# Hybrid attention block: logits of both heads of a pair from 64-row products, and another order of query ranges

## The chip, the core and the metric

The kernel runs on one core of one Trainium2 chip. The metric is the device time of one execution in microseconds (us). Five kinds of work appear in the profile: PE (TensorE matmuls), PEld (TensorE weight loads, which overlap PE), DVE (VectorE), ACT (ScalarE), POOL (GpSimd); SP is the queue that issues most DMAs. Lines such as L103 are lines of the kernel before; L103 is the helper through which most ordered instructions are recorded, so groups there are told apart by their tiles (`p`, `z`, `wt`, `av`).

## The reference

One layer on a (1, 1024, 1024) residual stream, 16 heads of 64 dimensions. What matters here is the attention branch, for each head and with the strictly causal mask `s < t`:

```
proj = h @ w_in            # q, k, v, z_a, u, z_b, m_a, m_b, each 1024 wide
z    = q @ k.T * 64**-0.5                                  # logits
A[t,s] = sigmoid(z_ts) * prod_{s<j<t} (1 - sigmoid(z_tj))  # stick breaking
p_a  = ((A @ v) * silu(z_a)) @ w_branch_a
```

Beside it runs a pooling branch (`u`, `z_b`, `w_branch_b`). Both are gated by `sigmoid(m_a)` and `sigmoid(m_b)`, summed, projected by `w_out`, added to `x`, and normed.

## The kernel before, in words

All inputs are float32. A product keeps the accuracy by splitting each operand in a high and a low part (type fp32r, "hi" and "lo"), and adding hi·hi, hi·lo and lo·hi in the same PSUM bank; that is three TensorE products of 128 rows and up to 512 columns for each 128 rows of depth.

The sequence is kept in reversed order, so that query block `qb` (128 queries) meets the keys from `qb*128` to the end, a width W of 1024, 896, 768, 640, 512, 384, 256 or 128 columns. A unit of attention is (p, h, t): one of 8 head pairs p, head h of the pair, query range t of two blocks (256 queries). W is cut in chunks of up to 512 columns, so a head has 4, 4, 2 and 2 chunks in t = 0, 1, 2, 3: four of 512 columns, five of 384, two of 256 and one of 128.

For each chunk `z_items` (it begins near L800) makes:

- the logits in a PSUM bank with the tag `z` (two banks);
- on ACT two sigmoids out of the bank, `om` = sigmoid(-z) (L819) and `be` = sigmoid(z) (L820);
- on POOL the causal mask of the first 128 columns of both (L824);
- after the last chunk of a block, on DVE, the running product of `om` (the scan, L826), and, put off until the next `flush`, `be` times the shifted running product (an ordered multiplication, recorded under L103). `be` then holds the attention weights of 128 queries.

`turn` transposes these weights 128x128 at a time on TensorE (`wt`, two PSUM banks with the tag `tr`), copies them to hi and lo (L845 on ACT, L846 on DVE) and flushes what was put off. `product` multiplies them with v (`av`), and `finish` (L870 to L876) adds up the parts, multiplies with silu(z_a) and stores to DRAM (`ga_d`).

A logit product of one head has only 64 rows of depth. The kernel before fills all 128 rows: for head 0 the tile `q0` holds q-hi in rows 0 to 63 and q-lo in rows 64 to 127; `kh` holds k-hi twice, above and below; `kl` holds k-lo in one half and zeros in the other. Then q0·kh is hi·hi + lo·hi in one product, and q0·kl is hi·lo. So a chunk of a head takes two products. Making these tiles takes moves from one half of the partitions to the other: 3 DMAs for each half-sequence of q (`use_q`), 5 for each of k (`use_k`), all issued on SP by `move` (L697), and 4 memsets on POOL (L678).

Between these pieces stand the projections. `fill(n)` emits n steps of the generator `projections`, each three products of 512 columns (`p`). Each pair has the k, the q, 0 to 2 gate and the z_a column tiles. `step` interleaves the logits of the units that come due, the transposes and av products of the current unit, and a share of the 70 steps of each pair (`QUANTA`, `SHARE`). The logits of a unit are made three units ahead (`LEAD`), and units are taken in the order `HT_ORDER`: (0,0), (0,2), (1,0), (1,2), (0,1), (0,3), (1,1), (1,3). Everything that is emitted through `order` in this stage keeps its program order on its engine; the rest (sigmoids, scans, copies) is placed by a scheduler at build time.

Of the kernel before, what the change touches and what calls it, by code (L numbers as in the profile page):

```python
# [30 lines left out]
Z_TAGS = ("z",)  # L31
# [26 lines left out]
def block_kernel(ctx, tc, a, out):  # L58
# [613 lines left out]
    with pool("at") as at:  # L672
        pair = {}

        klz = [atz.tile([P, 2, S], F32R, name=f"kl{i}") for i in range(2)]
        for t_ in klz:
            for h in range(2):
                gp.memset(t_[64 * (1 - h):64 * (1 - h) + 64, h].bitcast(F32), 0.0)  # L678

        def pair_tiles(p, use):  # L680

            def tile_(tag, shape, dt=F32R, pl=atz):
                return pl.tile([P] + shape, dt, tag=tag, bufs=2, name=f"{tag}_{p}")

            if use is use_k:
                pair[p] = dict(kh=tile_("kh", [2, S]), kl=klz[p % 2])
            elif use is use_q:
                pair[p]["q"] = [tile_(f"q{h}", [S]) for h in range(2)]
            elif use is use_za:
                pair[p].update(vv=tile_("vv", [8, 2, 2, HD], pl=at), za=tile_("za", [S], F32, at))  # L690
# [5 lines left out]
        def move(dst, src):  # L696
            nc.sync.dma_start(dst.bitcast(F32), src.bitcast(F32))  # L697

        def low(name, ps, hi):
            lo = atz.tile([P, 512], F32R, tag="lo", bufs=1, name=name)  # L700
            order(v.tensor_sub)(lo, ps, hi.bitcast(F32))
            return lo

        def use_q(p, sh, ps):
            (q0, q1), sl = pair[p]["q"], slice(sh * 512, sh * 512 + 512)
            act.copy(q0[:, sl], ps)
            lo = low(f"qlo{p}_{sh}", ps, q0[:, sl])
            move(q1[half(1), sl], q0[half(1), sl])
            move(q1[half(0), sl], lo[half(1)])
            move(q0[half(1), sl], lo[half(0)])  # L710

        def use_k(p, sh, ps):
            kh, kl, sl = pair[p]["kh"], pair[p]["kl"], slice(sh * 512, sh * 512 + 512)
            act.copy(kh[:, 0, sl], ps)

            def rest():
                lo = low(f"klo{p}_{sh}", ps, kh[:, 0, sl])
                for h in range(2):
                    move(kl[half(h), h, sl], lo[half(h)])
                move(kh[half(1), 1, sl], kh[half(1), 0, sl])  # L720
                move(kh[half(0), 1, sl], kh[half(1), 0, sl])
                move(kh[half(1), 0, sl], kh[half(0), 0, sl])

            behind.append(rest)
            if p == 0:
                flush()
# [71 lines left out]
        z_tags = cycle(Z_TAGS)  # L798

        def z_items(u):  # L800

            p, h, t = u
            st = pair[p]
            rows = unit_rows[u] = []
            for qb in (2 * t, 2 * t + 1):
                n0 = qb * P
                W = S - n0
                om = atz.tile([P, S], F32, tag="om", bufs=2, name=f"om{p}_{h}_{qb}")
                g = t // 2
                be = at.tile([P, S - 512 * g], F32, tag=f"be{g}", bufs=NBE[g], name=f"be{p}_{h}_{qb}")  # L810
                nch = (W + 511) // 512
                b0 = 0
                for i in range(nch):
                    n = -(-((W - b0) // P) // (nch - i)) * P
                    zp = bank(next(z_tags), f"z{p}_{h}_{qb}_{i}")
                    ks, qsl = slice(n0 + b0, n0 + b0 + n), slice(n0, n0 + P)
                    mm(zp[:, :n], st["q"][h][:, qsl], st["kh"][:, h, ks], start=True, stop=False)
                    mm(zp[:, :n], st["q"][h][:, qsl], st["kl"][:, h, ks], start=False, stop=True)
                    act.activation(om[:, b0:b0 + n], zp[:, :n], AF.Sigmoid, scale=-0.125)  # L819
                    act.activation(be[:, b0:b0 + n], zp[:, :n], AF.Sigmoid, scale=0.125)  # L820
                    b0 += n
                    if i == 0:
                        for tl, fill in ((om, 1.0), (be, 0.0)):
                            gp.affine_select(out=tl[:, :P], in_=tl[:, :P], pattern=[[1, P]], compare_op=ALU.is_gt, fill=fill, base=0, channel_multiplier=-1)  # L824
                    if i == nch - 1:
                        v.tensor_tensor_scan(om[:, :W], om[:, :W], om[:, :W], 1.0, ALU.mult, ALU.min)  # L826
                        behind.append(lambda be=be, om=om, W=W: order(v.tensor_mul)(be[:, 1:W], be[:, 1:W], om[:, :W - 1]))
                        rows.append(be)
# [54 lines left out]
        ahead = {}  # L883
        for i, u in enumerate(units):
            ahead.setdefault(i - LEAD[u[2]], []).append(u)
# [7 lines left out]
        def n_z(u):  # L893
            return 4 if u[2] < 2 else 2
# [9 lines left out]
        def av_items(u):  # L904
            c = chunks.index((u, u[2]))
            for kp in range(u[2], 4):
                turn_next()
                product(u, kp, *turned_[c])
                turned_[c] = None
                c += 1  # L910
                if kp == 3:
                    finish(u)
                yield

        def first_items():
            for _ in range(DEPTH):
                turn_next()
                yield

        def step(zus, i, quanta):  # L920

            zs = [(g, n) for g, n in ((z_items(zu), n_z(zu)) for zu in zus)]
            items = [g for _, g in sorted(((k + 0.5) / n, j) for j, (g, n) in enumerate(zs) for k in range(n))]
            items = [zs[j][0] for j in items]
            main, n_main = (first_items(), DEPTH) if i == -1 else (av_items(units[i]), 4 - units[i][2]) if i >= 0 else (None, 0)
            n = max(n_main, len(items))
            groups = [[] for _ in range(n)]
            for k, g in enumerate(items):
                groups[(2 * k + 1) * n // (2 * len(items))].append(g)
            for k in range(n_main):  # L930
                groups[(2 * k + 1) * n // (2 * n_main)].append(main)
            done = 0
            for k, group in enumerate(groups):
                for g in group:
                    next(g)
                upto = quanta * (k + 1) // n
                fill(upto - done)
                done = upto
            for g in [main] + [g for g, _ in zs]:
                assert g is None or next(g, None) is None  # L940
            if i < 0:
                flush()
# [3 lines left out]
        early_ = sorted(s_ for s_ in ahead if s_ < 0)  # L946
        for n, s_ in enumerate(early_):
            step(ahead[s_], s_, FIRST[1] * (n + 1) // len(early_) - FIRST[1] * n // len(early_))
        for p in range(NP):
            used = 0  # L950
            for k in range(8):
                upto = QUANTA[p] * sum(SHARE[:k + 1]) // sum(SHARE)
                step(ahead.get(p * 8 + k, []), p * 8 + k, upto - used)
                used = upto
                if p * 8 + k == max(ahead):
# [3 lines left out]
                    ga = load_ga(0, range(NP - 1))  # L959
        pinned[0] = False  # L960
# [143 lines left out]
```

## Time and profile before

| what | value |
|---|---|
| three runs | 1209.69, 1210.95, 1212.34 us; median 1210.95 us |
| profiled execution, first to last instruction | span 1210.3 us (its own time; 0.7 us under the median) |
| PE busy | 1199.2 us, 99% of the span |
| PEld busy | 1002.5 us, 83% |
| DVE, ACT, POOL busy | 756.5, 531.6, 187.2 us |
| mean granted TensorE clock | 0.999 |
| attention stage | first logit product at 415.8 us, last at 991.4 us |

The page says how long each engine was busy. A matmul row's mean time is longer than the distance from one matmul to the next, since matmuls are pipelined; the timeline's start times give the distance. Rows of the weight-load track show when the weights of a product were loaded; in a steady stream that is while the product ahead of it runs.

### The profile page before, as it was taken

Reading aid. Unit: us, or ns where it says so; the run is one execution under the profiler, and the core shown is the slowest. Engines: PE = TensorE matmul, PEld = TensorE weight load, DVE = VectorE, ACT = ScalarE, POOL = GpSimd, SP = SyncE. Lnnn points to the kernel's source line nnn. Section 1 sums busy time; section 2 is a strip of 40 time slices with the busy share of each in tenths; the row PEclk is TensorE's granted clock in tenths of the full one; section 3 lists DMA queues with packets and bytes.
Section 4 is the critical chain, followed back from the end, with each engine's and each line's share of the span. In section 5 each row is a group of like instructions: output and inputs, shape, how many; then the busy total and the mean of one; then the engine's idle time right before and its main releaser. Section 6 shows DMA issues by size and latency. Waiting matters only on the chain.

```text
span 1210.3 us, 16177 instructions
## 1 busy us (share of the span) xinstructions
PE 1199.2 (99%) x5746; PEld 1002.5 (83%) x5746; DVE 756.5 (63%) x1050; ACT 531.6 (44%) x1008; POOL 187.2 (15%) x360
## 2 busy tenths in 40 slices
PE   8999999999999999999999999999999999999997
PEld 7888878888888888888888888888888888888886
DVE  5764483677510286767868677686777853785643
ACT  5564331334301255655555555655555643232211
POOL 1000000001221333212222222222221210000001
PEclk9999999999999999999999999999999999999999
DMA  9649995626847632442635325353343344975622
GB/s 358 255 171 325 328 356 207 209 87 225 309 148 120 191 91 76 124 122 86 170 109 156 113 80 153 110 157 118 102 134 101 99 131 167 353 272 170 216 67 83
DMA packets 81955, 207.14 MB, mean 171 GB/s; under 512 B 10449, under 2 KB 23889, under 8 KB 79698
## 3 DMA queue, kind: packets, MB, share of 16 engines
q1 hardware_dynamic: 73666, 191.23, 49.2%
q10 hardware_dynamic: 8208, 14.88, 3.3%
q8 instruction: 45, 0.74, 0.2%
q14 instruction: 36, 0.29, 0.1%
HBM read 138.96 MB, written 50.34 MB: 156 GB/s over the span
## 4 chain that ended last, share of the span: by engine, by line
PE 88%; DMA 5%; issue 3%; DVE 2%; ACT 1%; POOL 0%; POOLq 0%; ACTq 0%; DVEq 0%; SPq 0%
PE p L103 34%; PE pb L103 7%; PE wzb L103 7%; PE pa L103 7%; PE o L103 6%; PE z L103 6%; PE av L103 5%; PE wt L103 5%; PE v L103 4%; PE ua L103 3%; DMA wl_d<-l_raw 2%; DMA l_raw<-in_w_in 2%; PE u L103 2%; PE wm L103 1%; DVE l_raw L156 1%
## 5 line engine op out<-in xcount | busy, mean ns | idle before, releaser
L103 PE MATMUL p<-hT,w 128*128 128x512 f32 x1920 | 480.0, 391 | 0.5 <-ACT m_sg L201 0.5
L103 PEld LDWEIGHTS p<-hT,w 128*128 128x128 f32 x1920 | 355.2, 188 | 74.7 <-ACT m_sg L201 1.0
L826 DVE TENSOR_TENSOR_SCAN om<-om 128x512 f32<-128x512 f32 (+7 forms) x128 | 175.8, 1373 | 124.9 <-ACT om L819 69.4
L819 ACT ACTIVATE om<-z 128x512 f32<-128x512 f32 (+2 forms) x192 | 94.5, 492 | 155.9 <-PE z L103 133.5
L824 POOL TENSOR_SCALAR_AFFINE_SELECT om<-om 128x128 f32<-128x128 f32 x128 | 56.3, 440 | 346.5 <-ACT om L819 287.0
L846 DVE TENSOR_TENSOR wt<-wt,wt 128x512 fp32r<-128x512 f32 (+1 forms) x160 | 99.3, 621 | 16.1 <-ACT wt L845 15.5
L845 ACT CAST wt<-wt 128x512 fp32r<-128x512 f32 (+1 forms) x160 | 88.2, 551 | 48.1 <-PE wt L103 47.9
L103 PE MATMUL av<-wt,vv 128*128 128x512 f32 x320 | 106.4, 414 | 0.0
L103 DVE TENSOR_TENSOR be<-be,om 128x511 f32<-128x511 f32 (+7 forms) x128 | 95.1, 749 | 1.1 <-POOL be L824 0.7
L820 ACT ACTIVATE be<-z 128x512 f32<-128x512 f32 (+2 forms) x192 | 94.1, 490 | 0.0
L103 PE MATMUL pa<-ga,wa 128*128 128x512 f32 x384 | 89.6, 389 | 0.1
L103 PE MATMUL o<-wo,mhl 128*128 128x512 f32 (+1 forms) x408 | 89.6, 377 | 0.0
L103 PE MATMUL wt<-ident,be 128*128 128x128 f32 x576 | 89.4, 273 | 0.0
L103 PE MATMUL v<-wv,hT 128*128 128x512 f32 x384 | 87.8, 390 | 0.5 <-DVE vo L611 0.5
L103 PE MATMUL wzb<-hT,wzb 128*128 128x512 f32 x384 | 87.2, 389 | 0.0
L103 PE MATMUL pb<-gb,wb 128*128 128x512 f32 x384 | 87.2, 389 | 0.0
L103 PEld LDWEIGHTS v<-wv,hT 128*128 128x128 f32 x384 | 71.9, 188 | 16.2 <-DVE vo L611 1.4
L103 PEld LDWEIGHTS o<-wo,mhl 128*128 128x128 f32 x408 | 73.5, 188 | 14.1
L103 PEld LDWEIGHTS pa<-ga,wa 128*128 128x128 f32 x384 | 72.0, 188 | 15.4 <-DVE wa L118 0.5
L103 PEld LDWEIGHTS wzb<-hT,wzb 128*128 128x128 f32 x384 | 72.1, 188 | 14.9
L103 PEld LDWEIGHTS pb<-gb,wb 128*128 128x128 f32 x384 | 72.1, 188 | 14.9
L103 PEld LDWEIGHTS wt<-ident,be 128*128 128x128 f32 x576 | 70.2, 141 | 11.6
(130 smaller groups left out, 1364.5 us busy)
## 6 DMA issues: line engine op xcount, KB each, us to landing
w_raw<-in_w_in SPq DMA_DIRECT2D x40, 512.0 KB, 4.7
l_raw<-in_w_in SPq DMA_DIRECT2D x32, 512.0 KB, 5.2
wl_d<-l_raw SPq DMA_DIRECT2D x32, 512.0 KB, 5.7
w<-wl_d SPq DMA_DIRECT2D x32, 512.0 KB, 3.8
v_d<-vo SPq DMA_DIRECT2D x16, 512.0 KB, 5.2
vv<-v_d SPq DMA_DIRECT2D x8, 1024.0 KB, 5.3
wa_raw<-in_w_branch_a SPq DMA_DIRECT2D x16, 512.0 KB, 4.7
wa<-in_w_mod SPq DMA_DIRECT2D x7, 1024.0 KB, 6.4
```

The source lines that it names most:

```text
L103: ins = op(*args, **kw)
L156: v.tensor_sub(raw.bitcast(F32R), raw, hi.bitcast(F32))
L819: act.activation(om[:, b0:b0 + n], zp[:, :n], AF.Sigmoid, scale=-0.125)
L820: act.activation(be[:, b0:b0 + n], zp[:, :n], AF.Sigmoid, scale=0.125)
L824: gp.affine_select(out=tl[:, :P], in_=tl[:, :P], pattern=[[1, P]], compare_op=ALU.is_gt, fill=fill, base=0, channel_multiplier=-1)
L826: v.tensor_tensor_scan(om[:, :W], om[:, :W], om[:, :W], 1.0, ALU.mult, ALU.min)
L845: act.copy(wt[:, 0, :off], pt[:, :off])
L846: v.tensor_sub(wt[:, 1, :off], pt[:, :off], wt[:, 0, :off].bitcast(F32))
```

## The change

The logits of both heads of a pair are made together. `use_q` and `use_k` keep q-hi, q-lo, k-hi, k-lo as they come out of the projection, head 0 in partitions 0 to 63 and head 1 in 64 to 127. A chunk of both heads is six products of 64 rows, hi·hi, lo·hi, hi·lo, each for head 0 in the upper half of the array's rows and for head 1 in the lower half, in two PSUM banks. The moves, the zeroed tiles and the POOL memsets go. Query ranges are taken in the order 0, 3, 1, 2, in each both heads one after the other; the logits of the next range of both heads are made during the current one, instead of three units ahead. Transposes run two chunks ahead of the av products over the whole stage (`main_items`), and the share of projection steps of each range is 15, 18, 17, 24 instead of equal eighths.

```diff
-HT_ORDER = ((0, 0), (0, 2), (1, 0), (1, 2), (0, 1), (0, 3), (1, 1), (1, 3))
-LEAD = {0: 3, 1: 3, 2: 3, 3: 3}
+T_ORDER = (0, 3, 1, 2)
+HT_ORDER = tuple((h, t) for t in T_ORDER for h in range(2))
 NBE = (4, 4)
-SHARE = (7,) * 8
+SHARE = (15, 18, 17, 24)
...
-        klz = [atz.tile([P, 2, S], F32R, name=f"kl{i}") for i in range(2)]
-        for t_ in klz:
-            for h in range(2):
-                gp.memset(t_[64 * (1 - h):64 * (1 - h) + 64, h].bitcast(F32), 0.0)
...
         def use_q(p, sh, ps):
-            (q0, q1), sl = pair[p]["q"], slice(sh * 512, sh * 512 + 512)
-            act.copy(q0[:, sl], ps)
-            lo = low(f"qlo{p}_{sh}", ps, q0[:, sl])
-            move(q1[half(1), sl], q0[half(1), sl])
-            move(q1[half(0), sl], lo[half(1)])
-            move(q0[half(1), sl], lo[half(0)])
+            (hi, lo), sl = pair[p]["q"], slice(sh * 512, sh * 512 + 512)
+            act.copy(hi[:, sl], ps)
+            order(v.tensor_sub)(lo[:, sl], ps, hi[:, sl].bitcast(F32))
...
-        def z_items(u):
+        def z_items(p, t):
+
+            (kh, kl), (qh, ql) = pair[p]["k"], pair[p]["q"]
...
-                    zp = bank(next(z_tags), f"z{p}_{h}_{qb}_{i}")
+                    zp = [bank("z", f"z{p}_{h}_{qb}_{i}") for h in range(2)]
                     ks, qsl = slice(n0 + b0, n0 + b0 + n), slice(n0, n0 + P)
-                    mm(zp[:, :n], st["q"][h][:, qsl], st["kh"][:, h, ks], start=True, stop=False)
-                    mm(zp[:, :n], st["q"][h][:, qsl], st["kl"][:, h, ks], start=False, stop=True)
-                    act.activation(om[:, b0:b0 + n], zp[:, :n], AF.Sigmoid, scale=-0.125)
-                    act.activation(be[:, b0:b0 + n], zp[:, :n], AF.Sigmoid, scale=0.125)
+                    for j, (q_, k_) in enumerate(((qh, kh), (ql, kh), (qh, kl))):
+                        for h in range(2):
+                            mm(zp[h][:, :n], q_[half(h), qsl], k_[half(h), ks], start=j == 0, stop=j == 2)
+                    for h in range(2):
+                        act.activation(om[h][:, b0:b0 + n], zp[h][:, :n], AF.Sigmoid, scale=-0.125)
+                        act.activation(be[h][:, b0:b0 + n], zp[h][:, :n], AF.Sigmoid, scale=0.125)
...
+        def main_items():
+            for c in range(len(chunks)):
                 turn_next()
+                if c >= DEPTH:
+                    use_chunk(c - DEPTH)
                 yield
...
+        def step(nxt, cur, quanta):
+
+            events = []
+            if nxt:
+                z, n = z_items(*nxt), n_z(nxt[1])
+                events += [((k + 0.2) / (n + 0.8), 0, z) for k in range(n)]
+            if cur:
+                n = 2 * (4 - cur[1])
+                events += [((k + 0.5) / n, 1, main) for k in range(n)]
```

Three places show what this does to the engines' orders. The first is TensorE, at the logits of query blocks 2 and 3 (range t = 1) of a pair. The names are `z_<head>_<block>_<chunk>`, `p_<half>`, `wt` (transposes) and `av`. Before:

```order
L103 MATMUL p_0_4965<-hT,w_13_4766 128x512 x6
L103 MATMUL z_0_2_0_4974<-kh_3899,q_2_4070 128x384
L103 MATMUL z_0_2_0_4974<-kl_2932,q_2_4070 128x384
L103 MATMUL p_0_4965<-hT,w_13_4766 128x512 x6
L103 MATMUL z_0_2_1_4989<-kh_3899,q_2_4070 128x384
L103 MATMUL z_0_2_1_4989<-kl_2932,q_2_4070 128x384
L103 MATMUL wt_1_0_0_4995<-ident,be_1_0_4775 128x128 x2
```

And in the change:

```order
L101 MATMUL z_0_2_0_5003<-kh_3854,qh_3993 128x384
L101 MATMUL z_1_2_0_5004<-kh_3854,qh_3993 128x384
L101 MATMUL z_0_2_0_5003<-kh_3854,ql_3994 128x384
L101 MATMUL z_1_2_0_5004<-kh_3854,ql_3994 128x384
L101 MATMUL z_0_2_0_5003<-kl_3855,qh_3993 128x384
L101 MATMUL z_1_2_0_5004<-kl_3855,qh_3993 128x384
L101 MATMUL p_1_5023<-hT,w_13_4720 128x512 x12
L101 MATMUL z_0_2_1_5036<-kh_3854,qh_3993 128x384
L101 MATMUL z_1_2_1_5037<-kh_3854,qh_3993 128x384
```

Two products for one head have become six for two heads, the heads taking turns. There are 96 such groups in place of 192 pairs of products, and each stands between products of 128 rows (or 128-row transposes).

The second place is DVE, at the logits of range t = 0 of the following pair, from the last scan of block 0 to the weights of block 1 (`om` is the scan, `be` the multiplication that makes the weights, `tp` an addition in `finish`, `wt` the low part of transposed weights). Before, for head 0:

```order
L826 SCALAR_TENSOR_TENSOR om_0_1_4626<-om_0_1_4626 128x896
L872 TENSOR_TENSOR tp_3_4649<-av_0_3_4646,tp_3_4649 64x256
L734 TENSOR_TENSOR za_4608<-p_0_4610,za_4608 128x512
L826 SCALAR_TENSOR_TENSOR om_0_4_4676<-om_0_4_4676 128x512
L846 TENSOR_TENSOR wt_1_1_3_4693<-wt_1_1_3_4688,wt_1_1_3_4693 128x512
L103 TENSOR_TENSOR be_0_1_4627<-be_0_1_4627,om_0_1_4626 128x895
```

And in the change, for both heads:

```order
L801 SCALAR_TENSOR_TENSOR om_0_1_5464<-om_0_1_5464 128x896
L801 SCALAR_TENSOR_TENSOR om_1_1_5465<-om_1_1_5465 128x896
L822 TENSOR_TENSOR wt_1_2_3_5549<-wt_1_2_3_5544,wt_1_2_3_5549 128x512
L101 TENSOR_TENSOR kl_5436<-p_0_5437,kh_5435 128x512
L101 TENSOR_TENSOR be_0_1_5466<-be_0_1_5466,om_0_1_5464 128x895
L101 TENSOR_TENSOR be_1_1_5467<-be_1_1_5467,om_1_1_5465 128x895
```

The scans of both heads now stand next to each other, and the weights of head 0 come after the scan of head 1. The transposes that need them, `wt_0_0_0` of the next pair, stand after 15 `p` products, four transposes, two av products and 9 more `p` products on TensorE, counted from the last logits of block 1.

The third place is ACT at the logits of block 2. Before, two sigmoids of one head follow each other (`om`, `be`), and the second of the two banks takes the next chunk. In the change:

```order
L691 CAST qh_4926<-p_0_4928 128x512
L793 ACTIVATE om_0_2_4999<-z_0_2_0_5003 128x384
L794 ACTIVATE be_0_2_5001<-z_0_2_0_5003 128x384
L793 ACTIVATE om_1_2_5000<-z_1_2_0_5004 128x384
L794 ACTIVATE be_1_2_5002<-z_1_2_0_5004 128x384
L793 ACTIVATE om_0_2_4999<-z_0_2_1_5036 128x384
```

Both banks are now filled at once, and four sigmoids empty them before the next group can begin.

More of the change, by code (lines that the diff above doesn't have):

```diff
@@ L685, in pair_tiles @@
             if use is use_k:
-                pair[p] = dict(kh=tile_("kh", [2, S]), kl=klz[p % 2])
+                pair[p] = dict(k=[tile_(n, [S]) for n in ("kh", "kl")])
             elif use is use_q:
-                pair[p]["q"] = [tile_(f"q{h}", [S]) for h in range(2)]
+                pair[p]["q"] = [tile_(n, [S]) for n in ("qh", "ql")]
             elif use is use_za:
@@ L693, in half @@
             return slice(64 * h, 64 * h + 64)
[L696 to L702, printed above, removed]
-        def use_q(p, sh, ps):
-            (q0, q1), sl = pair[p]["q"], slice(sh * 512, sh * 512 + 512)
-            act.copy(q0[:, sl], ps)
-            lo = low(f"qlo{p}_{sh}", ps, q0[:, sl])
-            move(q1[half(1), sl], q0[half(1), sl])
-            move(q1[half(0), sl], lo[half(1)])
-            move(q0[half(1), sl], lo[half(0)])
-        def use_k(p, sh, ps):
[L713 to L724, printed above, removed]
+        def use_q(p, sh, ps):
+            (hi, lo), sl = pair[p]["q"], slice(sh * 512, sh * 512 + 512)
+            act.copy(hi[:, sl], ps)
+            order(v.tensor_sub)(lo[:, sl], ps, hi[:, sl].bitcast(F32))
+        def use_k(p, sh, ps):
+            (hi, lo), sl = pair[p]["k"], slice(sh * 512, sh * 512 + 512)
+            act.copy(hi[:, sl], ps)
+            behind.append(lambda: order(v.tensor_sub)(lo[:, sl], ps, hi[:, sl].bitcast(F32)))
             if p == 0:
@@ L882, in block_kernel @@
         units = [(p, h, t) for p in range(NP) for h, t in HT_ORDER]
-        ahead = {}
-        for i, u in enumerate(units):
-            ahead.setdefault(i - LEAD[u[2]], []).append(u)
+        pairs = [(p, t) for p in range(NP) for t in T_ORDER]
         proj = projections()
@@ new lines, in main_items, with use_chunk @@
+                yield
+            for c in range(len(chunks) - DEPTH, len(chunks)):
+                use_chunk(c)
+            yield
+        def use_chunk(c):
+            u, kp = chunks[c]
+            product(u, kp, *turned_[c])
+            turned_[c] = None
+            if kp == 3:
+                finish(u)
+        main = main_items()
+        def step(nxt, cur, quanta):
[6 more added lines that the diff above has]
+                events += [((k + 0.5) / n, 1, main) for k in range(n)]
@@ L932, in step @@
             done = 0
[L933 to L936, printed above, removed]
+            for at_, _, g in sorted(events, key=lambda e: e[:2]):
+                upto = int(quanta * at_)
                 fill(upto - done)
                 done = upto
[L939 to L942, printed above, removed]
+                next(g)
@@ L944, in block_kernel @@
+            fill(quanta - done)
+            if nxt:
+                assert next(z, None) is None
         fill(FIRST[0])
         pinned[0] = True
-        early_ = sorted(s_ for s_ in ahead if s_ < 0)
-        for n, s_ in enumerate(early_):
-            step(ahead[s_], s_, FIRST[1] * (n + 1) // len(early_) - FIRST[1] * n // len(early_))
+        step(pairs[0], None, FIRST[1])
+        flush()
         for p in range(NP):
             used = 0
-            for k in range(8):
+            for k in range(4):
```

61 lines of the change are left out of this document (19 added, 42 removed).

## The prediction, made before the result was known

> **What bounds the kernel now.** I read the page's busy shares first, then the windows of single pairs, then the waits of the attention stage.
>
> ```profile
> span 1210.3 us, 16177 instructions
> PE 1199.2 (99%) x5746; PEld 1002.5 (83%) x5746; DVE 756.5 (63%) x1050; ACT 531.6 (44%) x1008; POOL 187.2 (15%) x360
> ```
>
> ```profile
> 438.00:511.00 73.00, 73.00 (x374) 61.64 (x372) 54.35 (x76) 42.62 (x90) 22.06 (x38) 1.00 0.35 97
> 876.00:949.00 73.00, 73.00 (x373) 61.60 (x372) 53.24 (x74) 41.58 (x90) 15.56 (x36) 1.00 0.40 119
> ```
>
> ```profile
> PE p L103 <- ACT m_sg L201: 0.5, 1, 0.5
> ```
>
> The window rows give PE, PEld, DVE, ACT, POOL busy in one pair's 73 us: PE all of it, DVE 54, ACT 42. Between 391 and 1030 us PE waited once, for 0.5 us. So the stage lasts as long as its TensorE stream: what is added to the stream is added to the time, and what is taken from DVE, ACT, SP or the DMAs gains nothing. A busy row doesn't say how dense the stream is, so the costs below are distances between starts.
>
> **What a logit product costs now.** The tile view of `z` counts the products (the other operand's row has the same counts), the chain has a long plain run, and three pieces of the timeline show starts.
>
> ```profile
> L103 PE MATMUL z<-kh,q x192: 220/333/389, 415.8 to 991.3; 128*128 128x384 f32 x80, 128*128 128x512 f32 x64, 128*128 128x256 f32 x32, 128*128 128x128 f32 x16
> ```
>
> ```profile
> 216.69 87.04 PE wzb L103 x384
> ```
>
> ```profile
> 512.88 0.39 PE L103 MATMUL z<-kh,q 128*128 128x512 f32 x1
> 513.11 0.39 PE L103 MATMUL z<-kl,q 128*128 128x512 f32 x1
> 513.34 0.60 PE L103 MATMUL wt<-ident,be 128*128 128x128 f32 x4
> 513.69 0.71 PE L103 MATMUL av<-wt,vv 128*128 128x512 f32 x2
> 514.24 1.55 PE L103 MATMUL p<-hT,w 128*128 128x512 f32 x6
> ...
> 517.81 0.33 PE L103 MATMUL z<-kh,q 128*128 128x384 f32 x1
> 517.98 0.34 PE L103 MATMUL z<-kl,q 128*128 128x384 f32 x1
> 518.15 0.60 PE L103 MATMUL wt<-ident,be 128*128 128x128 f32 x4
> ```
>
> ```profile
> 991.34 0.22 PE L103 MATMUL z<-kh,q 128*128 128x128 f32 x1
> 991.40 0.28 PE L103 MATMUL z<-kl,q 128*128 128x128 f32 x1
> ```
>
> 87.04/384 is 0.227 us for 512 columns. The logits keep that pace: 0.23 at 512, 0.17 at 384, 0.06 at 128, in proportion to the columns, and going into and out of them costs nothing. One pass over the logits of all heads has 64x512 + 80x384 + 32x256 + 16x128 = 73,728 columns, that is 144 x 0.227 = 32.7 us. Before there are two passes: 65.3 us.
>
> **Term 1, the products.** After the change there are three passes, with both heads at once if the two halves of the array run side by side. Then they last 3 x 32.7/2 = 49.0 us, which is **-16.3 us**. One by one they last 98.0 us, +32.7. No row shows two products side by side, since all products here but two are of 128 rows; these are the bounds. I take the first: the heads use different rows, different weights and different banks, and alternate in the order. In groups of 128 columns (8 of 96) the pace may be set by weight loads: the last two rows above show a load and its product every 0.06, so two loads make 0.11 against 0.06, and 8 x 3 x 0.06 = **+1.4 us**.
>
> **Term 2, going in and out.** The logits now stand in 96 groups, each between products of 128 rows: 192 changes. The only products of fewer rows in the trace are the spreads of `c`, `crow`, of one row, near the start.
>
> ```profile
> 8.71 1.24 PE L103 MATMUL wm<-praw,wt_raw 128*128 128x256 f32 x5
> 9.88 1.98 PE L103 MATMUL crow<-crow,ones 1*128 1x512 f32 x4
> 11.79 3.72 PE L103 MATMUL wm<-praw,wt_raw 128*128 128x256 f32 x16
> 15.35 7.07 PE L103 MATMUL wm<-praw,wt 128*128 128x256 f32 x32
> 22.25 0.93 PE L103 MATMUL xt<-ident,x 128*128 128x128 f32 x7
> ```
>
> ```profile
> 9.14 0.41 PEld L103 LDWEIGHTS wm<-praw,wt_raw 128*128 128x128 f32 x2
> 9.88 0.29 PEld L103 LDWEIGHTS crow<-crow,ones 1*128 1x128 f32 x2 [0.33 <-issue]
> 10.41 0.18 PEld L103 LDWEIGHTS crow<-crow,ones 1*128 1x128 f32 x1 [0.24 <-issue]
> 10.85 0.18 PEld L103 LDWEIGHTS crow<-crow,ones 1*128 1x128 f32 x1 [0.24 <-issue]
> 11.79 0.51 PEld L103 LDWEIGHTS wm<-praw,wt_raw 128*128 128x128 f32 x3 [0.76 <-issue]
> ```
>
> The run of 32 `wm` products gives their pace, (22.25 - 15.35)/32 = 0.216. Five from 8.71 end at 9.79, but `crow` begins at 9.88: 0.09 late. The second `crow` load starts at 9.88 + 0.29 - 0.18 = 9.99 and the fourth at 10.85, so a product takes 0.43, and four from 9.88 end at 11.60; `wm` begins at 11.79: 0.19 late. Sixteen from there would end at 15.24; the next begin at 15.35: 0.11 late. Together 0.39 us are lost on one trip in and out, and the rows say "issue": nothing the profile shows was awaited. I read it as two parts, each twice. The stream empties (0.09), and then the first weights load with nothing running (0.11, the distance of the first two `crow` loads), where otherwise the load stands beside the product ahead.
>
> [...]
>
> Carried over to 64 rows: emptying 2 x 0.09. The loads exposed are fp32r loads, which cannot take longer than the 0.06 of the rows at 991 us, against 0.11 for the fp32 loads of `crow`; 2 x 0.06. And the second head's weights load after the first head's, so its stream ends up to 0.06 later. That is 0.35 per group; its bounds are 0.18 (emptying alone) and 0.39 (as `crow`), below both 0 if 64 rows need no change of state. 96 x 0.35 = **+33.6 us** (17.3 to 37.4; rival B is 0).
>
> [...]
>
> **Term 3, the shorter lead.** Logits used to be three units ahead; now the last logits of range 0 stand just ahead of their first transposes. TensorE has 15 + 9 `p` products (5.4 us) and four transposes with two av products (0.9, as from 513.34 to 514.24) between them, 6.3 us, and 0.15 for leaving the group. Against it stands this chain on DVE, by the stage's groups by shape:
>
> ```profile
> L819 ACT ACTIVATE om<-z 128x384 f32<-128x384 f32 x80 | 39.4, 492 | 57.3 <-PE z L103 54.7 <-issue 1.6 <-ACT wt L845 0.7
> ```
>
> ```profile
> L846 DVE TENSOR_TENSOR wt<-wt,wt 128x512 fp32r<-128x512 f32 x94 | 63.3, 673 | 9.3 <-ACT wt L845 9.0
> L826 DVE TENSOR_TENSOR_SCAN om<-om 128x896 f32<-128x896 f32 x16 | 32.3, 2017 | 1.1 <-ACT om L819 0.8
> L103 DVE TENSOR_TENSOR be<-be,om 128x895 f32<-128x895 f32 x16 | 17.5, 1094 | 0.0
> L103 DVE TENSOR_TENSOR klo<-p,kh 128x512 fp32r<-128x512 f32 x14 | 9.5, 680 | 0.0
> ```
>
> Sigmoid 0.49, two scans 4.03, a `wt` low part 0.67, `be` 1.09: 6.3 us, and 0.68 more where a k low part stands between, as in the order shown. So TensorE arrives about when the weights do, and waits up to 0.5 us in the pairs with the k part: **+2 us** over the seven pairs that follow another. Bounds 0 and 5 (0.7 in each). The other ranges have some microseconds of room.
>
> **What is worth nothing.** 128 moves and four memsets go:
>
> ```profile
> kh<-kh SPq DMA_DIRECT2D x48, 128.0 KB, 3.7
> kl<-klo SPq DMA_DIRECT2D x32, 128.0 KB, 3.7
> q<-qlo SPq DMA_DIRECT2D x32, 128.0 KB, 2.4
> q<-q SPq DMA_DIRECT2D x16, 128.0 KB, 3.4
> ```
>
> They delayed other loads on SP, but PE waited for no load in the stage, so this is hidden under the TensorE stream (0; if that cover went, a load of weights would come earlier, not later). DVE and ACT do the same operations as before. The two banks of `z` are now filled together, and the next group waits for four sigmoids, 4 x 0.49 = 2.0 us, where 12 `p` products (2.7 us) stand between at the tightest: 0.
>
> **Sum.** -16.3 + 1.4 + 33.6 + 2 = +20.7. On the profiled 1210.3 (0.7 below the median, which I add back) this gives 1231.0, and 1231.7 against the median: **1232 us**, slower by 1.7%. The case's own range is 1213 (0.18 per group, no wait) to 1238.5 (0.39, 5 us of waits).
>
> **Rivals.**
>
> A is this forecast, chance 0.60.
>
> B: changing to 64 rows costs nothing. The place is the same 192 borders, and the change is faster as soon as a group's way in and out costs less than (16.3 - 1.4 - 2)/96 = 0.13 us. With 0.06 at most, for the second head's late start, the sum is -16.3 + 1.4 + 2 + 3 (half of 5.8) = -10, **1201 us**. For it: half of the rows is not one row, and the transposes between products of other kinds show no loss. Against it: `crow` waited for nothing and still lost 0.39, three times that limit. Chance 0.22, of which 0.04 near the limit, where the time is within 0.2% (2.4 us, about what a measurement of this kernel tells from no change).
>
> C: the change doesn't do what it says, and the halves run one after the other. The groups lose 0.30 (no late second head) and the products gain nothing: 32.7 + 28.8 + 2 = +63, **1274 us**; with free borders 1246. For it: no row shows two products at once. Against it: the heads share neither rows nor banks. Chance 0.13.
>
> D: the shorter lead decides. If ACT takes up a group's sigmoids 2 us later than I count, since it now has four in a row, TensorE waits 2 us at the first transposes of each of the eight pairs, 16 in place of term 3: 20.7 - 2 + 16 = +35, **1246 us**. It decides once the chain of term 3 is more than 0.2 us longer than the 6.5 us of cover. For it: DVE is at 54 of 73 us, in bursts. Against it: ACT is idle 30 of 73 us. Chance 0.05.
>
> **Numbers.** The likeliest is 1232. The range 1199 to 1252 holds A, nearly all of B, D, and C with free borders; outside stay C with its borders (about 0.1) and B's best (0.05). Faster by over 0.2%: B without its margin, 0.18. Within: 0.05. Slower: 0.77.
>
> **What would show it.** In the changed profile, the first `z` of a group should start about 0.1 us later than the `p` ahead of it allows, with its weight load at the same time, and the `p` behind likewise (term 2; none of it is B). The `z` of head 1 should start within 0.06 of head 0's, and the next product of head 0 one product time later (term 1; two product times is C). PE waits for `be` should be a few, under 1 us, at the first transposes of a pair (term 3; long or many is D). PE should stay busy with a pair's period about 2.6 us over 73. The forecast is wrong if the borders lose less than 0.13 us or the pairs of products take over 1.5 times one.

## The result, and the profile after

| | before | after |
|---|---|---|
| median | 1211.45 us (1209.69 to 1212.34) | 1262.43 us (1259.51 to 1264.86) |
| profiled execution, span | 1210.3 us | 1263.1 us |
| last `p` before the first logits to the first `pa` behind the stage | 613.5 us | 665.6 us |
| mean granted TensorE clock | 0.999 | 0.991 |

The change makes the kernel slower: ratio 1.0423, 95% interval 1.0403 to 1.0444. The forecast was slower by 20.7 us; it is 51 us. The spans of the profiled executions differ by 52.8 us, and 52.0 of that lie in the attention stage. The page of the changed kernel, its span and busy shares:

```profile
span 1263.1 us, 16295 instructions
PE 1231.6 (98%) x5938; PEld 980.3 (78%) x5938; DVE 769.9 (61%) x1050; ACT 531.8 (42%) x1008; POOL 183.2 (15%) x356
```

PE is busy 32 us longer and idle 20 us more. One pair, as the window view shows it (columns as in the prediction):

```profile
518.00:596.00 78.00, 76.47 (x399) 58.70 (x399) 54.55 (x75) 42.29 (x90) 16.52 (x36) 1.00 0.27 92
```

A pair's period went from 73 to 78 us, and in it PE is no longer busy throughout. What PE waited for is in the view of waits (us in total, times, longest):

```profile
PE av L101 <- DVE tp L848: 15.2, 8, 3.3
PE p L101 <- ACT m_sg L199: 2.5, 1, 2.5
PE wt L101 <- DVE be L101: 1.9, 3, 1.4
```

Before, the stage had one wait, 0.5 us, for `m_sg`. The third row is what the prediction had looked for; the first, eight times larger, is something that it did not look at.

**The borders.** The timeline of TensorE and of its weight loads around one group of 512 columns:

```profile
548.72 4.26 PE L101 MATMUL p<-hT,w 128*128 128x512 f32 x18
552.91 0.50 PE L101 MATMUL z<-kh,qh 64*128 64x512 f32 x2
553.25 0.40 PE L101 MATMUL z<-kh,ql 64*128 64x512 f32 x2
553.48 0.40 PE L101 MATMUL z<-kl,qh 64*128 64x512 f32 x2
553.81 0.55 PE L101 MATMUL wt<-ident,be 128*128 128x128 f32 x3
```

```profile
552.91 0.19 PEld L101 LDWEIGHTS z<-kh,qh 64*128 64x128 f32 x2 [0.35 <-issue]
553.02 0.19 PEld L101 LDWEIGHTS z<-kh,ql 64*128 64x128 f32 x2
553.25 0.19 PEld L101 LDWEIGHTS z<-kl,qh 64*128 64x128 f32 x2
553.81 0.31 PEld L101 LDWEIGHTS wt<-ident,be 128*128 128x128 f32 x3 [0.37 <-issue]
```

The view joins the two heads' products in one row ("x2"): in the trace they start 3 ns apart, so the halves do run side by side. But the first loads stand at the same time as the first products (552.91 and 552.91, again at 553.81): nothing was loaded ahead. From 552.91 the next product comes after 0.34 (0.11 over a product of 0.23), then after 0.23, then the border out after 0.33 (0.10 over). The medians over all groups of 512 columns, by starts: 0.318 from the last `p` to the first `z` (0.091 over 0.227), 0.332 to the second, 0.230 to the third, 0.323 to a following `p` (0.096 over), and 0.337 to the `p` after that (0.110 over). Together that is 0.40 us per group.

**The wait for a bank.** Two units later, TensorE and DVE:

```profile
558.76 0.60 PE L101 MATMUL wt<-ident,be 128*128 128x128 f32 x4
560.89 0.58 PE L101 MATMUL av<-wt,vv 128*128 128x512 f32 x2 [1.53 <-DVE tp L848]
```

```profile
554.96 1.23 DVE L801 TENSOR_TENSOR_SCAN om<-om 128x512 f32<-128x512 f32 x1 [1.44 <-POOL om L798]
556.54 1.29 DVE L801 TENSOR_TENSOR_SCAN om<-om 128x512 f32<-128x512 f32 x1 [0.36 <-POOL om L798]
557.75 0.53 DVE L822 TENSOR_TENSOR wt<-wt,wt 128x384 fp32r<-128x384 f32 x1
558.20 0.67 DVE L101 TENSOR_TENSOR be<-be,om 128x511 f32<-128x511 f32 x1
558.80 0.41 DVE L848 TENSOR_TENSOR tp<-av,tp 64x256 f32<-64x256 f32 x1
559.13 0.67 DVE L101 TENSOR_TENSOR be<-be,om 128x511 f32<-128x511 f32 x1
559.73 0.68 DVE L822 TENSOR_TENSOR wt<-wt,wt 128x512 fp32r<-128x512 f32 x1
560.33 1.31 DVE L848 TENSOR_TENSOR tp<-av,tp 64x256 f32<-64x256 f32 x3
```

`av` products accumulate in one of two PSUM banks, and a bank comes free when the two additions of `finish` (`tp`, L848 of the changed kernel) have read it. The units of range 3 are short, one av step each, and the new order puts both heads of it side by side with range 1 behind: three units within three steps, on two banks. The third, the first unit of range 1, needs the bank that head 0 of range 3 had two steps earlier. Its additions stand on DVE behind two scans of 512 columns, each of which waits for the mask on POOL (1.44 and 0.36 us), and behind the weights and low parts that follow; the second addition starts at 560.33, the waiting product at 560.89. That product's weights also came late (its load, at 560.86, is put down to `wt` on ACT); which of the two held it up, the first experiment tells. This happens once in every pair. The view counts such a wait from the modelled end of the product ahead; by the distances between starts the eight waits are 17.2 us.

**The clock.** The window view for two stretches just after such waits (the last three columns are granted clock, DMA share and GB/s), and the first of them on the timeline:

```profile
482.00:485.50 3.50, 3.50 (x13) 2.43 (x13) 2.66 (x5) 1.64 (x4) 1.18 (x3) 0.55 0.23 95
717.00:721.00 4.00, 3.97 (x14) 2.83 (x15) 1.94 (x4) 1.64 (x4) 2.38 (x5) 0.61 0.12 37
```

```profile
481.83 0.58 PE L101 MATMUL av<-wt,vv 128*128 128x512 f32 x2 [3.32 <-DVE tp L848]
...
483.60 2.63 PE L101 MATMUL p<-hT,w 128*128 128x512 f32 x6
...
557.38 1.53 PE L101 MATMUL p<-hT,w 128*128 128x512 f32 x6
```

Six `p` products took 1.53 us elsewhere and 2.63 here. In the trace some 30 `p` products of the stage start 0.427 us after the one ahead instead of 0.227, all within 5 us behind a wait. To price this, take every distance between two starts in the 5 us behind each of the ten longest waits, less the stage's median distance for the same products in the same neighbourhood, and add up: six times that is 1.51 to 1.73 us, four times 0.02 to 0.04. It happens whole or not at all, and makes 9.4 us. The trace's record of the granted clock shows the same directly: six stretches in the stage at 0.50, each 3.41 us long, from 482.35, 717.87, 874.88, 953.39, 1031.89 and 1055.79 us on (the view of 482.35:485.76 gives 0.50); half of 3.41 is 1.7. The four executions agree: two with a granted clock of 0.991 took 1264.3 and 1264.9 us, two with 0.995 took 1259.5 and 1260.6.

So the 52.0 us are, by this reading: products and borders about 20, the bank 15.2, the half clock 9.4, `m_sg` and `be` 3.9 more than before, and some 3 or 4 that no view assigns; with the bank counted by starts (17.2) it is under 2. The experiments test these parts.

### The profile page after: what moved, and what is told of

Read it like the earlier page. It is cut to its first block, busy times and chain, and to the rows that moved or that the text cites. A ratio compares the mean times of both kernels' runs of the same rounds, so it can differ in the third digit from the quotient of the medians.

```text
span 1263.1 us, 16295 instructions
## 1 busy us (share of the span) xinstructions
PE 1231.6 (98%) x5938; PEld 980.3 (78%) x5938; DVE 769.9 (61%) x1050; ACT 531.8 (42%) x1008; POOL 183.2 (15%) x356
## 4 chain that ended last, share of the span: by engine, by line
PE 73%; issue 15%; DVE 5%; POOL 3%; DMA 3%; ACT 1%; POOLq 0%; SPq 0%; DVEq 0%; ACTq 0%
PE p L101 23%; PE pb L101 7%; PE wzb L101 7%; PE v L101 7%; PE o L101 6%; PE pa L101 5%; PE u L101 4%; PE z L101 4%; PE av L101 3%; PE wt L101 3%; PE ua L101 3%; POOL om L798 1%; DVE be L101 1%; PE wm L101 1%; DMA m<-sb_d 1%
## 5 line engine op out<-in xcount | busy, mean ns | idle before, releaser
L101 PE MATMUL p<-hT,w 128*128 128x512 f32 x1920 | 492.8, 400 | 2.5 <-ACT m_sg L199 2.5
L101 PEld LDWEIGHTS p<-hT,w 128*128 128x128 f32 x1920 | 355.9, 191 | 96.0 <-issue 16.8
L801 DVE TENSOR_TENSOR_SCAN om<-om 128x896 f32<-128x896 f32 (+7 forms) x128 | 176.4, 1399 | 89.7 <-ACT om L793 50.8
L101 PE MATMUL av<-wt,vv 128*128 128x512 f32 x320 | 106.3, 413 | 15.2 <-DVE tp L848 15.2
L101 DVE TENSOR_TENSOR be<-be,om 128x895 f32<-128x895 f32 (+7 forms) x128 | 97.0, 789 | 0.3
L101 PE MATMUL wt<-ident,be 128*128 128x128 f32 x576 | 91.6, 275 | 2.0 <-DVE be L101 1.9
L101 PEld LDWEIGHTS wt<-ident,be 128*128 128x128 f32 x576 | 71.0, 140 | 27.6 <-issue 8.4
L101 PE MATMUL pa<-ga,wa 128*128 128x512 f32 x384 | 89.9, 390 | 1.2 <-DVE s L971 1.2
L101 PE MATMUL o<-wo,mhl 128*128 128x512 f32 (+1 forms) x408 | 89.6, 377 | 0.0
L101 PE MATMUL wzb<-hT,wzb 128*128 128x512 f32 x384 | 87.2, 389 | 0.0
L101 PE MATMUL pb<-gb,wb 128*128 128x512 f32 x384 | 87.2, 389 | 0.0
L101 PE MATMUL v<-wv,hT 128*128 128x512 f32 x384 | 87.2, 389 | 0.0
L101 PEld LDWEIGHTS pa<-ga,wa 128*128 128x128 f32 x384 | 71.9, 188 | 16.9 <-issue 1.6
L101 PEld LDWEIGHTS o<-wo,mhl 128*128 128x128 f32 x408 | 73.4, 188 | 14.2 <-DVE mhl L116 0.2
L101 PEld LDWEIGHTS wzb<-hT,wzb 128*128 128x128 f32 x384 | 72.1, 188 | 15.0
L101 PEld LDWEIGHTS pb<-gb,wb 128*128 128x128 f32 x384 | 72.1, 188 | 15.0
L101 PEld LDWEIGHTS v<-wv,hT 128*128 128x128 f32 x384 | 72.1, 188 | 15.0
```

The costliest lines, as they stand in the source:

```text
L101: ins = op(*args, **kw)
L801: v.tensor_tensor_scan(o_[:, :W], o_[:, :W], o_[:, :W], 1.0, ALU.mult, ALU.min)
```

## The experiments

The theory after the comparison: (1) 64-row products with their borders cost about 20 us; (2) the bank that `tp` frees late costs the rest, by its wait and by the clock behind it. Two rivals: the borders are much dearer than reckoned and the waits only fill slack; or the products are a gain, and the new order itself is the loss.

### ACT empties the bank

One copy by ACT takes the whole bank to SBUF; DVE adds from there.

```diff
             act.copy(tp[r], av[64:128, 0])
+            if h == 0:
+                both["sc", t] = at.tile([P, 2, 256], F32, tag="sc", bufs=2, name=f"sc{p}_{t}")
+            sc = both["sc", t]
+            act.copy(sc[r], av[0:64])
             for i in range(2):
-                v.tensor_add(tp[r], av[0:64, i], tp[r])
+                v.tensor_add(tp[r], sc[r, i], tp[r])
```

> The changed kernel, but ACT copies the whole av bank to SBUF, so that the bank is free without DVE; DVE adds from SBUF. Theory (T): of the 52 us, some 20 are the borders of the 64-row groups less the products saved, and some 30 are TensorE waiting for av banks that DVE frees late (17 us on TensorE's starts) with the half clock that follows such waits (8 us) and small waits. Then the av waits go and most of the half clock with them: 1238 us (1233 to 1245). Rival (R1): the waits are only where a slower stream shows; what is taken away there comes back elsewhere, and the time stays above 1252 us.

Measured: 1243.64 us (1243.45 to 1243.91), ratio to before 1.0263 (1.0248 to 1.0278). The waits of the stage are now these:

```profile
PE p L101 <- ACT m_sg L199: 4.1, 1, 4.1
PE wt L101 <- DVE be L101: 1.9, 3, 1.4
PE wt L101 <- DVE wt L822: 0.9, 1, 0.9
```

No row for `av` is left. So it was the bank, and not the weights of the product, that TensorE waited for. 18.8 us are gone by the medians (22.3 in the stage of the profiled executions), more than the 15.2 of the wait although 2.5 us of other waits are new: the clock behind it goes too, and of six half clocks one is left, behind `m_sg`. The waits filled no slack.

### The same order with 128-row products

Here two products of 128 rows per head stand in place of three of 64. They add the logits of both heads, so the logits are wrong; the count and form of the products are the ones of the kernel before.

```diff
-                    for j, (q_, k_) in enumerate(((qh, kh), (ql, kh), (qh, kl))):
-                        for h in range(2):
-                            mm(zp[h][:, :n], q_[half(h), qsl], k_[half(h), ks], start=j == 0, stop=j == 2)
+                    for h in range(2):
+                        mm(zp[h][:, :n], qh[:, qsl], kh[:, ks], start=True, stop=False)
+                        mm(zp[h][:, :n], qh[:, qsl], kl[:, ks], start=False, stop=True)
```

> The changed kernel in its own order, but each head's logits by two products of 128 rows, as many and as long as in the kernel before (they add up both heads, so the logits are others than the reference's). T: the borders (33.6) and the slow small groups (1.4) go, the third pass saved (16.3) comes back: 18.7 us less, 1244 us; since TensorE then reaches the av products earlier, waits may take up to 10 of it: 1244 to 1254. Rival (R2): the 64-row products gain by themselves and the order of ranges alone costs; then the time rises by 16 to about 1278 us.

Measured: 1238.43 us (1234.68 to 1240.83), ratio 1.021 (1.0187 to 1.0232). This is below the window. The wait for the bank is still there, `PE av L101 <- DVE tp L848` with 12.9 us in 8 times, but half clock follows three waits instead of six. The 64-row products are no gain.

### Both together

> Both edits: 128-row products (logits other than the reference's) and ACT frees the av bank. T: neither borders nor av waits are left, what stays is the short lead: 1213 to 1222 us, near the kernel before. R2: the order itself costs more than the av banks: above 1235 us.

Measured: 1223.94 us (1221.69 to 1224.96), ratio 1.0098 (1.008 to 1.0115), 2 us over the window. The four kernels make a table (medians, us):

| | bank freed by DVE | bank freed by ACT | difference |
|---|---|---|---|
| 64-row products | 1262.43 | 1243.64 | 18.8 |
| 128-row products | 1238.43 | 1223.94 | 14.5 |
| difference | 24.0 | 19.7 | |

The parts add nearly: 64 rows cost 19.7 to 24.0, the larger where the half clock takes its share, and the bank 14.5 to 18.8. Both rivals fall. With both gone 12 us over before were left, in which `m_sg` waits of 3.2 us, low-part and `be` waits of 3.4 and one of 1.5 in front of the output products stand in the view of waits.

### The border by itself

The kernel before, with one more product of 128 columns ahead of each chunk's logits, in the same bank, which the next product overwrites. Once with 64 rows, once, as a control, with 128:

```diff
+                    mm(zp[:, :P], st["q"][h][0:64, qsl], st["kh"][0:64, h, n0:n0 + P], start=True, stop=True)
                     mm(zp[:, :n], st["q"][h][:, qsl], st["kh"][:, h, ks], start=True, stop=False)
```

> The kernel before, with one more product ahead of each chunk's logits: 64 rows, 128 columns, into the same bank, overwritten by the product after it. It measures the border alone: 192 ways into 64 rows and out again, no other order, no third pass. T, with 0.29 per border pair (0.09 twice for emptying, 0.053 twice for a load with nothing running) and 0.057 for the product: 192 x 0.35 = 67 us, 1278 us (1268 to 1290). Rival, the border is free in this kernel and what the changed kernel loses there is something else in its groups: 192 x 0.057 = 11 us, 1222 us.

> The control: the same extra product with all 128 rows. Both theories: 192 x 0.057 = 11 us for the products themselves, 1223 us (1218 to 1228).

Measured: 1298.77 us (1297.06 to 1299.37), ratio 1.0722 (1.0703 to 1.0741), with 64 rows; 1233.61 us (1233.06 to 1234.05), ratio 1.0188 (1.017 to 1.0206), with 128. Both are above their windows. The stage grew by 86.4 us for 192 such products of 64 rows, 0.450 each, and by 22.4 for 192 of 128 rows, 0.117 each. TensorE and its loads around one of 64 rows (the joined row is the extra product and the first one of 128 rows behind it):

```profile
518.91 0.75 PE L103 MATMUL z<-kh,q 64*128 64x128 f32 x2
519.50 0.40 PE L103 MATMUL z<-kl,q 128*128 128x512 f32 x1
519.73 1.53 PE L103 MATMUL p<-hT,w 128*128 128x512 f32 x6
```

```profile
518.91 0.44 PEld L103 LDWEIGHTS z<-kh,q 64*128 64x128 f32 x2 [0.36 <-ACT be L821]
519.27 0.19 PEld L103 LDWEIGHTS z<-kl,q 128*128 128x128 f32 x1
```

The label `ACT be` on the first load marks the end of the last sigmoid that read the bank, at 518.73; the same 0.35 stands ahead of 109 other such loads with the label `issue`. The medians by starts: 0.319 into the extra product (0.092 over a `p`), 0.253 out of it (0.196 over its 0.057), and 0.335 for the product behind (0.108 over 0.227). That is 0.40 for one way in and out, with a single product of 64 rows between; 0.450 less 0.057 says 0.39. The border costs what `crow` lost, and it is the same for half the rows as for one row. Its parts are two of 0.09, read here as the stream emptying, and two loads of 0.11 in the open.

The control fits the 0.11. With all products of 128 rows, a product of 128 columns costs 0.117, not 0.057 (a quarter of 0.227), as it would if a load of weights takes about 0.11 and a product that is shorter than that doesn't cover the load of the next.

### One head after the other

The same six products, in another program order: three of head 0, then three of head 1.

```diff
-                    for j, (q_, k_) in enumerate(((qh, kh), (ql, kh), (qh, kl))):
-                        for h in range(2):
+                    for h in range(2):
+                        for j, (q_, k_) in enumerate(((qh, kh), (ql, kh), (qh, kl))):
```

> The changed kernel with the three products of head 0 first and then the three of head 1, in place of the heads taking turns. If products start in program order and only neighbours in the order can run side by side, a group lasts five product times in place of three (the last of head 0 beside the first of head 1): 2 x 16.3 = 33 us more on TensorE, less what it saves in waits for av banks, 1275 to 1295 us. Rival: the engine pairs what lies in the two halves whatever the order, and the time stays at 1262 us.

Measured: 1257.3 us (1255.69 to 1259.35), ratio 1.0377 (1.0359 to 1.0394). No slower than the change; the rival of that expectation was right. The timeline of this kernel, in the group that answers to the one above:

```profile
554.00 0.50 PE L101 MATMUL z<-kh,qh 64*128 64x512 f32 x2
554.33 0.40 PE L101 MATMUL z<-kh,ql 64*128 64x512 f32 x2
554.57 0.40 PE L101 MATMUL z<-kl,qh 64*128 64x512 f32 x2
```

In program order, in the built program too, the two hi·hi products stand three apart, yet they start 10 ns apart: the first product of head 1 overtook the second and third of head 0. So alternating the heads isn't what makes them run together. That this version is faster by 5 us (9.1 by the profiled executions, 1254.0 against 1263.1) has nothing to do with the borders: its waits are 3.0 us less in sum (the bank 10.6 in place of 15.2, two other rows 1.6 more), and half clock follows two waits instead of six, 3.3 us in place of 9.4. These two are the 9.1.

### Another share of projection steps

Range 1, which is taken third, gets 22 steps instead of 17, and range 2 gets 19: the `av` products come later against DVE.

```diff
-SHARE = (15, 18, 17, 24)
+SHARE = (15, 18, 22, 19)
```

> The changed kernel with other shares: 15, 18, 22, 19 in place of 15, 18, 17, 24, so that five more of 74 parts of the projection steps stand between the av products of range 1, where TensorE waits for the av bank of range 3, and five fewer in range 2. T: six av steps share about 4.7 more steps of 0.68 us, 0.5 us for each; the bank that is needed two av steps after it was filled gets about 1 us more. Of waits of 1.3 to 3.6 us some 7 us go, and most of the half clock behind them (up to 6): 1248 to 1256 us, unless the shorter range 2 makes new waits for weights there. R1 (waits only move): 1262 us.

Measured: 1247.91 us (1246.65 to 1248.39), ratio 1.0304 (1.0288 to 1.032), 0.1 us below the window. The waits of the stage:

```profile
PE wt L101 <- DVE be L101: 10.9, 8, 1.6
PE av L101 <- DVE tp L848: 2.1, 1, 2.1
```

Of 15.2 us for the bank 13.1 are gone, and 9.0 come back as waits for `be`, one per pair, because the share was taken from the range whose cover the first transposes of the next pair need. That DVE is late has only changed its place. Still 14.5 us were won by the medians, 15.6 in the stage of the profiled executions. These hold 4.1 of these waits, the 2.5 of `m_sg`, and of six half clocks five (9.4 to 1.5, that is 7.9). None of the new waits is over 1.6 us, and none is followed by half clock.

### Without the scans that stand ahead

The two scans of query block 4 are left out, so the attention weights of that block are wrong.

```diff
-                            v.tensor_tensor_scan(o_[:, :W], o_[:, :W], o_[:, :W], 1.0, ALU.mult, ALU.min)
+                            if qb != 4:
+                                v.tensor_tensor_scan(o_[:, :W], o_[:, :W], o_[:, :W], 1.0, ALU.mult, ALU.min)
```

> The changed kernel without the two scans (running products) of query block 4 in each pair, which stand on DVE, behind a wait for POOL, ahead of the additions that free the av bank of range 3; the weights of block 4 are wrong, TensorE's work is the same. T: the additions come some 3 us earlier (2 x 1.23 and the waits of 1.1 to 1.9 us for the mask), the waits for av banks fall from 15 us to under 4 and the half clock with them: 1238 to 1248 us. Rival: the bank is late because three units with two banks follow each other within three av steps and ACT and the transposes between them take that long; then the waits stay and the time is above 1256 us.

Measured: 1249.12 us (1246.17 to 1250.96), ratio 1.0313 (1.0294 to 1.0333), 1 us above the window.

```profile
PE av L101 <- DVE tp L849: 6.6, 7, 1.3
```

With 2.5 us less on DVE ahead of the additions the wait falls by more than half, and none of the seven is followed by half clock; the one that is left follows a wait of 2.7 us for `m_sg`. What stays, 6.6 us, shows that the scans are most of the delay and not all of it: three units still follow each other on two banks.

### The end of the stage

In the version in which ACT empties the bank, `m_sg` held TensorE up by 4.1 us. On ACT it stood behind these (timeline of that version):

```profile
1029.45 0.62 ACT L758 CAST ga<-gr 128x512 fp32r<-128x512 f32 x1 [0.54 <-DMA gr<-ga_d]
...
1032.81 0.62 ACT L758 CAST ga<-gr 128x512 fp32r<-128x512 f32 x1 [2.74 <-DMA gr<-ga_d]
1033.34 0.59 ACT L199 ACTIVATE m_sg<-p 128x512 f32<-128x512 f32 x1
```

The loads of the attention output (`gr`, cast to `ga`) are issued for the output products while the last pair still runs, and their casts hold up ACT. Three versions issue them behind the last `av` product in program order: the 64-row one with ACT emptying the bank, the same with shares 15, 18, 19, 22, and the 128-row one.

```diff
-                    ga = load_ga(0, range(NP - 1))
         next(main)
         pinned[0] = False
+        ga = load_ga(0, range(NP - 1))
```

> The version in which ACT empties the av banks, and besides the loads of the attention output of the first pairs (ga) are issued behind the last av product of the stage instead of before it. T: the 4.1 us that TensorE waits near the stage's end for the m_sg sigmoid come from ACT's queue, where m_sg stands behind casts that wait for these loads; moved behind, the wait and the half clock after it go, so 1243.6 - 4.1 - 1.5 = 1238 us (1236 to 1240). Rival: the output products that follow then wait for the loads instead, and the time stays at 1242 to 1245.

> As the run with late ga loads, with shares of projection steps 15, 18, 19, 22, which gives range 1 (the last but one taken) two more steps. T: the few be and low-part waits that are left (2.8 us) shift but do not go, so 1234 to 1240 us; with every wait gone the changed order would be at 1211 + 20 (three 64-row products in place of two of 128 rows) = 1231, so no setting of shares brings it to the kernel before. Rival: what is left over 1231 is a cost of the order itself, and the time stays at or above the run with late ga loads.

> The changed order with 128-row products (the logits add both heads and are wrong), ACT empties the av banks, ga loads late. T: with the borders and the waits both gone nothing of the change is left on TensorE but some 3 us of be and low-part waits: 1224 - 3.2 - 1.5 = 1219 us (1214 to 1220). Rival: the new order costs something that no wait shows, and the time stays at 1222 to 1225.

Measured:

| | us | ratio to before |
|---|---|---|
| 64 rows, late loads | 1236.48 (1236.01 to 1236.95) | 1.0207 (1.0192 to 1.0222) |
| the same, other shares | 1238.07 (1237.49 to 1238.42) | 1.0219 (1.0204 to 1.0235) |
| 128 rows, late loads | 1218.49 (1218.18 to 1220.76) | 1.0057 (1.0041 to 1.0074) |

The first won 7.2 us by the medians, 5.4 in the stage of the profiled executions: the wait of 4.1 and the half clock of 1.7 behind it, less a new wait of 0.2. Its waits are

```profile
PE wt L101 <- DVE be L101: 1.9, 3, 1.4
PE wt L101 <- DVE wt L822: 0.9, 1, 0.9
PE av L101 <- DVE wt L822: 0.2, 1, 0.2
```

and no half clock is left. The casts themselves still stand among the last pair's work, since the build places them by when they can run; but `m_sg` now comes after three of them instead of after all seven. The shares change nothing for the better, and this version doesn't tell its theory from its rival. The third is 7.4 us slower than before, and its view of waits lists 6.0 us in the stage, against 0.5 before: so the new order costs little but what the waits show. And 64 rows against 128, both with late loads, is 18.0 us by the medians, and 16.4 by the stages of the two profiled executions, in which the waits were read; with 3.0 us fewer waits on the side of the 64 rows the latter is 19.4. The starts say the same: summed over the 96 groups, from the last product ahead of each to the second behind it, it is 128.1 us with 64 rows and 108.4 with 128, that is 19.7. This is the price of the 64-row products with nothing else in the way. No version comes to the kernel before.

## Why the prediction was right and wrong

**The sign and the sum of terms 1 and 2 were right.** They made +18.7 us. The pairs of kernels that differ in the products alone give 24.0, 19.7 and 18.0 by the medians; set right for their waits and their half clock, some 18 to 21. By the starts of the 96 groups it is 19.7.

**Term 1 held.** The two heads start 3 ns apart, and the three passes take half of three. Rival C is refuted by that, not by the total, which came near its 1274 for other reasons. The prediction thought that the alternating order was part of it; the order of the heads doesn't matter. The small groups cost 0.4 us instead of 1.4. (Its remark that all products but two are of 128 rows miscounts: the trace before has four of one row, those of `crow`. Nothing rests on that.)

**Term 2 was right in kind and a little low**: on average a group pays 0.37, from (19.7 + 16.3 - 0.4)/96, in place of 0.35. Where projections stand on both sides it is 0.38 to 0.42, about the upper bound; where transposes follow it is less, 0.36 in groups of 512 columns. That the sum came so near is in part luck, since two of its pieces were misjudged, in opposite directions. The second head isn't late by 0.06, but by 0.003. And a load takes 0.11, not at most 0.06: the prediction read 0.06 as the length of a load from two products that start 0.06 apart. The row behind them in the same view shows the loss, which stands one product later (kernel before):

```profile
991.40 0.28 PE L103 MATMUL z<-kl,q 128*128 128x128 f32 x1
991.51 0.52 PE L103 MATMUL wt<-ident,be 128*128 128x128 f32 x3
```

By its columns the second product of 128 lasts 0.06 too (a quarter of 0.227), but the next one comes after 0.11. Rival B, a border that is free, is refuted by every run with 64 rows.

**Term 3 was right in its sum by luck**: 2 us were forecast for `be`, and 1.9 measured, in three waits at the first transposes of a pair. But 1.4 of them stand in the first pair (at 437.5 us), which the forecast left out; the seven pairs that follow another, for which it forecast the 2 us, have two waits of 0.3 and 0.2.

**The step that failed is "DVE and ACT do the same operations as before", under what is worth nothing.** The operations are the same; their order against TensorE's is not. The prediction asked of the new order only when the weights (`be`) arrive, and of PSUM only the two `z` banks. It never asked it of the two `av` banks, although the order of units, 0, 3, 1, 2, with one step for each head of range 3, could be read off the code, and an addition of `finish` stands in the DVE order of the kernel before, ahead of the prediction. This is 15.2 us of waits. The second thing it had no term for is the clock: six waits of 1.5 to 3.3 us on the engine that sets the end cost 1.5 to 1.7 us each beyond their length, 9.4 us in all. The third is the `m_sg` wait at the stage's end, 2.0 us more than before. Those three make 26.6 us of the 30 that the sum lacks (28.6 of 31 in the profiled executions, with the bank counted by starts).

Rival D had the right kind, a wait in each of the eight pairs that decides, and 1246 us, but another place (`be` instead of the bank) and 0.05 of the chance. D joined the forecast's borders with 16 us of waits, near the 15.2 of the bank, but had nothing for the clock behind them, and the range ended at 1252.

## What to carry to other kernels

By these numbers products that use half of the rows have to be many in a row to pay: a group of six saves 0.17 us (16.3/96) and its two borders cost 0.37 on average. When an order of work is changed, ask of every buffer with two copies how many of its users now follow each other, and which engine frees it behind what; that DVE was busy 54 of 73 us said nothing about this. And on the engine that sets the end, a wait can cost more than its length: here 13 of the 14 gaps of 2.3 us and more between the starts of two TensorE products were followed by half clock, at 1.4 to 1.7 us each.

## What the runs showed of the hardware

- With one head after the other, products in the two halves of the rows proceeded independently: a later one in the other half overtook two earlier ones (10 ns apart where the program has two products between; 3 ns apart with the heads taking turns).
- Going into products of fewer rows and back cost about 0.4 us between longer products of 128 rows, whether 1 row (`crow`, 0.39) or 64 rows were used, and whether one product (0.39 to 0.40) or six (0.38 to 0.42) stood between. Half of it or more is loads of 0.11 that weren't made ahead.
- A product of 128 columns with weights of its own, put between products of 128 rows, cost 0.117, not 0.057, and in the kernel before the loss shows one product later than the product that causes it (0.06, then 0.11, at 991.40).
- Half clock behind a wait cost 1.4 to 1.7 us each time, however long the wait was. In the stages of the change and of nine of its variants it followed 13 of the 14 gaps of 2.3 us and more between the starts of two products, 2 of the 7 gaps of 1.79 to 1.87 us, and none of 1.72 or less. In the stage each stretch is 3.41 us long, and in every trace with two or more such stretches they begin whole multiples of 3.413 us apart (in the changed kernel 69, 46, 23, 23 and 7 of them), so in these traces the clock changed on a fixed beat. Cut into the windows of that beat, all 13 windows in which TensorE stood still for 2.0 us or more were followed by half clock, and 2 of the 15 with 1.5 to 1.95 us. The one long gap without half clock, 2.7 us, lies across a border, with 1.9 us on one side. What decides between 1.5 and 1.95 us is open.
